# A two-layer decoder trunk: four emission delays, two step spacings of the norms, a shorter weight look-ahead and a fifth lead pair

## The chip, the cores and the metric

The kernel runs on one core of one Trainium2 chip. The metric is the device time of one execution in microseconds: 1768.06 us is the median of three runs before the change (1768.06, 1768.21, 1762.78). Matrix products run on TensorE (PE in the profile, its weight loads PEld), elementwise work on VectorE (DVE), ScalarE (ACT) and GpSimd (POOL); all transfers of weights are queued from SyncE (SP). Each engine works through its own instructions in order.

## The reference, cut to what matters

544 tokens (one prompt of 512 and eight groups of four) pass two layers. Each layer has a token mixer and a SwiGLU feed forward, with a norm ahead of each and behind each, all in float32:

```python
for i in range(DEPTH):                       # DEPTH = 2
    hn = rms_norm(x, mix_pre_norm[i])
    if i % N_MIXERS == 0:
        out, S, cbuf = gdn_mixer(hn, ...)    # gated DeltaNet, layer 0
    else:
        out, hs, cbuf = ssd_mixer(hn, ...)   # Mamba-2, layer 1
    x = x + rms_norm(out, mix_post_norm[i])
    hn = rms_norm(x, ffn_pre_norm[i])
    f = (silu(hn @ ffn_w_gate[i]) * (hn @ ffn_w_up[i])) @ ffn_w_down[i]
    x = x + rms_norm(f, ffn_post_norm[i])
```

D_MODEL is 1024 (8 tiles of 128 features), D_FF 2816 (22 tiles).

## The kernel before

Activations lie with features on the 128 partitions and tokens along the free axis, in two halves of 272 tokens, called hf0 and hf1 here. A float32 operand is split into a high and a low part, and one step of a product over 128 features is three matmuls: high activation by high weight (L238), low activation by high weight (L239), high activation by low weight (L240). Such a step is called a k-step below; the program has 3648 of them.

**Weights** come in pieces of 128x512 (256 KB). `fetch_to` moves a piece in over the SP queue into one of four buffers `wraw`, ACT writes its high part `wh` (L210) and DVE the difference `wl` (L211) into one of five buffer pairs `wspl`. `emit` writes a unit (one output tile of one half): before it writes the product with piece i, it calls `fetch_to(base+i+AHEAD)`, so that pieces up to i+AHEAD-1 have been written into the program by then.

**What sets the order.** The kernel is written out by a planner, `Flow`. It has a virtual time `now`, which each written product moves on, and a list of tasks (Python generators) that run when their due time has come. A task that yields (w, d) is due again d later. The order of writing gives a priority, and a scheduler then places the instructions of each engine; so the numbers in the change are no waits on the chip, they only set the order in which instructions stand on each engine.

**Norms.** Behind the last output tile of a half, `Post.finish` is started. It sums the squares over the features by small matmuls (`ms`, L345), runs a Newton iteration for the inverse root on DVE (L317 to L328, 11 small instructions), spreads the result over partitions (`dg` on DVE L334, `r` on PE L337), and then, for each of 8 tiles: `fw *= r` (DVE L444), `x += fw` (DVE L446, for every third tile POOL), and `pre.square`, which adds the tile's squares for the next norm (ACT, then DVE `acc` L373). Where a feed forward follows, `pre.square` also writes the split of the unnormalized x (`xh` ACT L307, `xl` DVE L308), and the factor r is applied behind the product. `Pre.end` then does sum, Newton and spread for the second norm; where a mixer follows, it writes the normalized tiles `xn` (DVE L409) and their splits `xh`, `xl` (L210, L211). Before hf1's products of the next stage can start, hf1's second norm must have come this far.

**Lead pairs.** A feed forward starts with NL gate and up pairs for hf0 alone, then the same NL pairs for hf1, with their weights fetched and split again; the remaining pairs do both halves with one fetch. While hf0's lead runs, hf1's norms are finished. The gated outputs of the lead lie in the tile `g1`, those of the others in `g2`.

**The DeltaNet mixer** (30 to 440 us) writes its projections for 32 tiles, and per head tasks beside them: `q_task`, `v_task`, `decay`, `scan`, `o_norm`, with start delays in virtual us.

Of the kernel before, what the change touches and what calls it, by code (L numbers as in the profile page):

```python
# [22 lines left out]
NC = SEQ // P  # L23
KFF = 22
NSQ = 5
AHEAD = 5
NL = 4
NZ = 2
ZLAG = 3
SLEAD = 3  # L30
FINE = 12
WIDE = 4
NH0 = 4
PACE = 5.0
LIVE = 3
RAWW = 3 + SEQ + NB * 7
# [48 lines left out]
def _program(nc, tc, io, es):  # L85
# [81 lines left out]
    flow = Flow()  # L167
# [109 lines left out]
    def emit(u, fine=False, wide=False):  # L277
# [7 lines left out]
        for i, s in enumerate(ws):  # L285
            fetch_to(base + i + AHEAD)
            if m < P:
# [92 lines left out]
    class Pre:  # L380
# [16 lines left out]

        def end(self):
            y = rsq(self.ss.sum(), 1e-6)
            yield 0.0, 1.0  # L400
            r = spread(y)
            st.ready[self.hf] = True
            if self.free:
                st.r[self.hf] = sqp.tile([P, H2], F32, tag="sq", name="r", bufs=NSQ)
                S.activation(out=st.r[self.hf], in_=r, func=AF.Copy)
                return
            for k in range(KD):
                t = sqp.tile([P, H2], F32, tag="sq", name="xn", bufs=NSQ)
                V.scalar_tensor_tensor(out=t, in0=self.x[:, k, :], scalar=self.w(k),  # L409
                                       in1=r, op0=ALU.mult, op1=ALU.mult)  # L410
                split(self.xh[:, k, :], self.xl[:, k, :], t)
# [5 lines left out]
    class Post:  # L417
# [17 lines left out]

        def finish(self, hf):
            y = rsq(self.ss[hf].sum(), self.e, None if self.extra is None else self.extra[:, half(hf)])
            yield 0.0, 1.0
            r = spread(y)
            x = st.x[hf]  # L440
            pre = self.pre(hf)
            for k in range(KD):
                f = self.fw(k, hf)
                V.tensor_tensor(out=f, in0=f, in1=r, op=ALU.mult)  # L444
                E = G if k % 3 == 2 else V
                E.tensor_tensor(out=x[:, k, :], in0=x[:, k, :], in1=f, op=ALU.add)  # L446
                pre.square(k)
                yield 0.0, 0.6
            yield from pre.end()

    def ab(tiles, operand, tail):
# [130 lines left out]
    def gdn():  # L582
# [88 lines left out]
        def decay(p):  # L671
            for h in (2 * p, 2 * p + 1):
                d = hd[h]
                gr = t544("gr")
                dma(gr, gd[h].partition_broadcast(P))
                yield 0.0, 1.5
                d.E = tokt("E")
                d.Es = sm.tile([32, 32], F32, tag="Es", name="Es", bufs=6)
                for c in range(NC):
                    V.scalar_tensor_tensor(out=d.E[:, c, :], in0=gr[:, chunk(c)], scalar=Gm[:, c, h:h + 1],  # L680
                                           in1=maskP, op0=ALU.subtract, op1=ALU.min)
                V.scalar_tensor_tensor(out=d.Es, in0=gr[0:32, SEQ:T], scalar=Gm[0:32, 4, h:h + 1], in1=maskS,
                                       op0=ALU.subtract, op1=ALU.min)
                yield 0.0, 1.0
            for d in hd[2 * p:2 * p + 2]:
                S.activation(out=d.E, in_=d.E, func=AF.Exp)
                S.activation(out=d.Es, in_=d.Es, func=AF.Exp)
                d.decay = True
# [190 lines left out]
        def q_after(m, Y):  # L879
            h = m  # L880
            d = hd[h]
            d.q = t544("qT")
            S.activation(out=d.q, in_=Y, func=AF.Silu)
            d.gr = t544("eg")
            dma(d.gr, egd[h].partition_broadcast(P))
            d.el = late.tile([P, 12], F32, tag="el", name="el")
            G.tensor_copy(out=d.el[:, 0:4], in_=d.gr[:, P - 1:SEQ:P])
            G.tensor_copy(out=d.el[:, 4:12], in_=d.gr[:, SEQ + TS - 1:T:TS])
            flow.start(q_task(h), 6.5)

        def q_task(h):
            d = hd[h]
            p, e = divmod(h, 2)
            q, r2 = d.q, pr[p].rk2[:, e, :]
            yield lambda: hasattr(d, "kps")
            qk = dbank("qk")
            for c in range(NC):
                PE.matmul(qk[:, chunk(c)], lhsT=d.k[:, chunk(c)], rhs=q[:, chunk(c)],
                          start=True, stop=True)
            for c in range(NC):  # L900
                V.scalar_tensor_tensor(out=d.E[:, c, :], in0=qk[:, chunk(c)], scalar=r2[:, c:c + 1],
                                       in1=d.E[:, c, :], op0=ALU.mult, op1=ALU.mult)

            sq = t544("qsq")
            S.activation(out=sq, in_=q, func=AF.Square)
            yield 0.9, 0.9
            if e == 0:
                pr[p].qs2 = sm.tile([P, H2], F32, tag="qs2", name="qs2", bufs=3)
            ps = dbank("qss")
            for hf in range(2):  # L910
                r0 = 64 * e + 32 * hf
                PE.matmul(ps[r0:r0 + 32, 0:H2], lhsT=cst[:, C_QQ:C_QQ + 32], rhs=sq[:, half(hf)],
                          start=True, stop=True)
            PE.matmul(ps[0:32, 288:320], lhsT=d.k[:, SEQ:T], rhs=q[:, SEQ:T], start=True, stop=True)
            V.tensor_copy(out=pr[p].qs2[64 * e:64 * e + 64], in_=ps[64 * e:64 * e + 64, 0:H2])
            V.scalar_tensor_tensor(out=d.Es, in0=ps[0:32, 288:320], scalar=r2[0:32, 4:5], in1=d.Es,
                                   op0=ALU.mult, op1=ALU.mult)
            V.tensor_tensor(out=q, in0=q, in1=d.gr, op=ALU.mult)
            yield 0.5, 1.5
            d.qe = True  # L920


        def v_after(m, Y):
            h = m - 16
            v = t544("vT")
            S.activation(out=v, in_=Y, func=AF.Silu)
            flow.start(v_task(h, v), 3.5)

        def v_task(h, v):
            d = hd[h]  # L930
            p, e = divmod(h, 2)
            yield lambda: hasattr(pr[p], "irk")
            irk = pr[p].irk[:, e, :]
            vt = dbank("vtok")
            for c in range(NC):
                PE.transpose(vt[:, chunk(c)], v[:, chunk(c)], ident)
            vs = dbank("vsm")
            PE.transpose(vs[0:32, 0:P], v[:, SEQ:T], ident)
            d.v = tokt("vs")
            V.tensor_tensor(out=d.v, in0=vt.rearrange("p (c k) -> p c k", k=P),  # L940
                            in1=irk[:, 0:NC].unsqueeze(2).to_broadcast([P, NC, P]), op=ALU.mult)
            d.vs = sm.tile([32, P], F32, tag="vs", name="vs", bufs=3)
            V.tensor_scalar(out=d.vs, in0=vs[0:32, 0:P], scalar1=irk[0:32, 4:5], scalar2=None,
                            op0=ALU.mult)
            yield 0.6, 1.2
            yield lambda: hasattr(pr[p], "Dt") and hasattr(d, "qe")
            yield lambda: live[0] < LIVE
            live[0] += 1
            d.o = d.q
            d.left = 2  # L950
            flow.start(scan(h))
            flow.start(sample(h))
# [3 lines left out]
        def ended(h):  # L956
            d = hd[h]
            d.left -= 1
            if d.left == 0:
                live[0] -= 1  # L960
                p = h // 2
                d.ended = True
                if hasattr(hd[h ^ 1], "ended"):
                    flow.start(o_norm(p), 4.0)

        def scan(h):
            d = hd[h]
# [143 lines left out]
        for u in units(start_first(tiles, xop, 1)):  # L1111
            n = names.get(id(u[0]))
            if n is not None and u[1] == 0 and n[0] == "k":
                h = int(n[1])
                if h >= 4:
                    flow.until(lambda: hasattr(hd[h - 4], "ended"))
                if h % 2 == 1 and h < 7:
                    flow.start(decay(h // 2 + 1), 5.0)
            emit(u)
        flow.drain()  # L1120
        conv.close("g")
# [32 lines left out]
    def ffn(layer, last, before, lx, items):  # L1154
        fx = ExitStack()
        ev = pool(f"f{layer}_e", 2, fx, side="right")
        g1 = pool(f"f{layer}_g1", 1, fx, side="right")
        gt = [[[g1.tile([P, NL, H2], F32R, name=f"ga{i}{j}")] for j in range(2)] for i in range(2)]

        def gated(hf, m):  # L1160
            return [(t[0][:, m, :] if m < NL else t[1][:, m - NL, :]) for t in gt[hf]]

# [19 lines left out]
        for m in range(KFF):  # L1182
            tiles += [([io["f_g"][layer, m]], gate_done(m)), ([io["f_u"][layer, m]], up_done(m))]
        for u in units(start_first(tiles, xop, 2 * NL)):
            flow.until(lambda: st.ready[u[1]])
            if u[1] and before is not None:
# [3 lines left out]
                for i in range(2):  # L1190
                    for j in range(2):
                        gt[i][j].append(g2.tile([P, KFF - NL, H2], F32R, name=f"gb{i}{j}"))
                st.updated = False
# [508 lines left out]
```

## Time and profile before

The page of the profile has the busy time of each engine; the trace behind it can be asked for waits and for stretches. The profiled execution is one of its own, with its own time.

| | |
|---|---|
| median of three runs | 1768.06 us |
| the profiled execution | 1778.71 us |
| its span, first to last instruction | 1776.9 us |
| mean granted clock of TensorE | 0.978 |
| DVE / ACT / POOL busy | 1162.0 / 818.0 / 110.2 us |
| weight pieces split, `wl` | 556 |

In rows of a group, "x" is the count, then busy us and the mean ns of one. In a waits row stand the total, the times and the longest. In a windows row each engine has its busy us and, in brackets, its instructions in that stretch; PEclk is the granted clock as a share of full speed. In a timeline row stand the start, the duration, the engine, the line, the instruction, and in square brackets how long the engine was idle before it and what ended that.

### The profile page before, as it was taken

Reading aid. Unit: us, or ns where it says so; the run is one execution under the profiler, and the core shown is the slowest. Engines: PE = TensorE matmul, PEld = TensorE weight load, DVE = VectorE, ACT = ScalarE, POOL = GpSimd, SP = SyncE. Lnnn points to the kernel's source line nnn. Section 1 sums busy time; section 2 is a strip of 40 time slices with the busy share of each in tenths; the row PEclk is TensorE's granted clock in tenths of the full one; section 3 lists DMA queues with packets and bytes.
Section 4 is the critical chain, followed back from the end, with each engine's and each line's share of the span. In section 5 each row is a group of like instructions: output and inputs, shape, how many; then the busy total and the mean of one; then the engine's idle time right before and its main releaser. Section 6 shows DMA issues by size and latency. Waiting matters only on the chain.

```text
span 1776.9 us, 37092 instructions
## 1 busy us (share of the span) xinstructions
PE 1697.0 (96%) x14127; PEld 1612.5 (91%) x14127; DVE 1162.0 (65%) x3069; ACT 818.0 (46%) x1824; POOL 110.2 (6%) x335
## 2 busy tenths in 40 slices
PE   4999999999899999999889999999999999999997
PEld 3888888899799999999777898999998999999996
DVE  6786858455876655324877897978458766665345
ACT  4754654436543333334555555556446433333242
POOL 0112121000000000000001110100001000000000
PEclk8989999999899999999989999999999999999998
DMA  5323323334354432225535544432344544444444
GB/s 141 104 64 100 88 69 96 106 104 145 114 175 145 143 108 90 83 80 143 181 95 150 160 134 137 142 116 74 134 137 137 179 143 141 139 149 131 125 138 130
DMA packets 163124, 220.87 MB, mean 124 GB/s; under 512 B 53185, under 2 KB 66049, under 8 KB 162433
## 3 DMA queue, kind: packets, MB, share of 16 engines
q1 hardware_dynamic: 162944, 218.49, 40.8%
q8 instruction: 111, 1.82, 0.4%
q14 instruction: 69, 0.56, 0.1%
HBM read 197.39 MB, written 21.04 MB: 123 GB/s over the span
## 4 chain that ended last, share of the span: by engine, by line
PE 88%; DVE 6%; ACT 2%; DMA 2%; issue 1%; POOL 0%; SPq 0%; DVEq 0%; ACTq 0%; POOLq 0%
PE mm L238 25%; PE mm L240 25%; PE mm L239 24%; DVE acc L373 1%; PE yd L1495 1%; PE yos L1386 1%; PE yo L1500 1%; PE su L1472 1%; DVE wl L211 1%; PE mm L247 1%; DVE fw L444 1%; PE r L337 1%; PE sc L985 1%; PE ms L345 1%; PE su L573 1%
## 5 line engine op out<-in xcount | busy, mean ns | idle before, releaser
L238 PE MATMUL mm<-xh,wh 128*128 128x272 f32 x2560 | 757.5, 296 | 8.2 <-ACT wh L210 5.1
L240 PE MATMUL mm<-xh,wl 128*128 128x272 f32 x2560 | 752.5, 294 | 2.7 <-DVE wl L211 2.7
L239 PE MATMUL mm<-xl,wh 128*128 128x272 f32 x2560 | 749.8, 293 | 0.0
L211 DVE TENSOR_TENSOR wl<-wr,wh 128x512 fp32r<-128x512 f32 (+1 forms) x556 | 375.8, 679 | 260.0 <-ACT wh L210 247.2
L210 ACT ACTIVATE wh<-wr 128x512 fp32r<-128x512 f32 (+1 forms) x556 | 344.7, 622 | 428.4 <-PE mm L239 377.5
L238 PEld LDWEIGHTS mm<-xh,wh 128*128 128x128 f32 x2560 | 488.8, 191 | 25.9 <-issue 8.0
L240 PEld LDWEIGHTS mm<-xh,wl 128*128 128x128 f32 x2560 | 488.2, 191 | 8.2 <-DVE wl L211 3.8
L239 PEld LDWEIGHTS mm<-xl,wh 128*128 128x128 f32 x2560 | 488.7, 191 | 3.7 <-issue 0.6
L238 PE MATMUL mm<-gb,wh 128*128 128x272 f32 x576 | 166.7, 291 | 0.0
L240 PE MATMUL mm<-gb,wl 128*128 128x272 f32 x576 | 164.9, 289 | 0.4 <-DVE wl L211 0.4
L239 PE MATMUL mm<-gb,wh 128*128 128x272 f32 x576 | 164.3, 288 | 0.0
L544 DVE SCALAR_TENSOR_TENSOR conv<-raw,cw,conv 128x512 f32<-128x512 f32 x144 | 106.8, 742 | 8.7 <-ACT conv L541 8.1
L238 PEld LDWEIGHTS mm<-gb,wh 128*128 128x128 f32 x576 | 108.4, 188 | 1.3 <-ACT wh L210 0.3
L240 PEld LDWEIGHTS mm<-gb,wl 128*128 128x128 f32 x576 | 107.7, 188 | 1.0 <-DVE wl L211 0.6
L239 PEld LDWEIGHTS mm<-gb,wh 128*128 128x128 f32 x576 | 107.8, 188 | 0.4
L1169 ACT ACTIVATE sg<-sg 128x272 f32<-128x272 f32 x88 | 37.7, 431 | 101.2 <-DVE sg L1168 100.6
L446 POOL TENSOR_TENSOR x<-x,fw 128x272 f32<-128x272 f32 x16 | 16.3, 1020 | 1070.4 <-DVE fw L444 561.0
L373 DVE TENSOR_TENSOR acc<-acc,sq 128x272 f32<-128x272 f32 x112 | 50.1, 448 | 45.9 <-ACT sq L366 45.3
L240 PE MATMUL mm<-yh,wl 128*128 128x272 f32 x256 | 73.8, 290 | 2.1 <-DVE wl L211 2.1
L239 PE MATMUL mm<-yl,wh 128*128 128x272 f32 x256 | 74.3, 291 | 1.2 <-DVE yl L308 1.2
L238 PE MATMUL mm<-yh,wh 128*128 128x272 f32 x256 | 73.9, 289 | 0.0
L210 ACT ACTIVATE gb<-sg 128x272 fp32r<-128x272 f32 x72 | 31.1, 432 | 92.8 <-DVE sg L1177 92.8
(399 smaller groups left out, 2428.9 us busy)
## 6 DMA issues: line engine op xcount, KB each, us to landing
wr<-f_d_in SPq DMA_DIRECT2D x110, 256.0 KB
wr<-f_g_in SPq DMA_DIRECT2D x104, 256.0 KB
wr<-f_u_in SPq DMA_DIRECT2D x104, 256.0 KB
wr<-g_w_in SPq DMA_DIRECT2D x64, 256.0 KB
wr<-s_w_in SPq DMA_DIRECT2D x48, 256.0 KB
wr<-s_wo_in SPq DMA_DIRECT2D x44, 256.0 KB
wr<-s_wz_in SPq DMA_DIRECT2D x36, 256.0 KB
ar<-ad SPq DMA_DIRECT2D x32, 272.0 KB
```

Source lines behind the costliest of these rows:

```text
L210: S.activation(out=hi, in_=src, func=AF.Copy)
L211: V.tensor_tensor(out=lo, in0=src, in1=hi.bitcast(F32), op=ALU.subtract)
L238: PE.matmul(ps, lhsT=h[:, k, :], rhs=ah(k0 + k), start=first and k == 0, stop=False)
L239: PE.matmul(ps, lhsT=h[:, k, :], rhs=al(k0 + k), start=False, stop=False)
L240: PE.matmul(ps, lhsT=lo[:, k, :], rhs=ah(k0 + k), start=False, stop=last and k == n - 1)
L247: PE.matmul(ps[0:64], lhsT=w[:, k, :], rhs=a(k), start=j == 0 and k == 0, stop=j == 1 and k == KD - 1)
L337: PE.matmul(r, lhsT=ones[0:TQ, :], rhs=dg.rearrange("p j t -> p (j t)"), start=True, stop=True)
L345: PE.matmul(ps[:, j:j + 1], lhsT=ss[:, q], rhs=sel, start=True, stop=extra is None)
L373: V.tensor_tensor(out=self.acc, in0=self.acc, in1=self.late, op=ALU.add)
L444: V.tensor_tensor(out=f, in0=f, in1=r, op=ALU.mult)
L544: V.scalar_tensor_tensor(out=Y[:, 0:SEQ], in0=R[:, j:j + SEQ], scalar=w[:, j:j + 1], in1=Y[:, 0:SEQ], op0=ALU.mult, op1=ALU.add)
L1169: S.activation(out=t, in_=t, func=AF.Silu)
```

## The change

Six parts, all in what the planner is told:

- AHEAD goes from 5 to 4: a piece is written into the program one piece later.
- NL goes from 4 to 5: each of the two feed forwards fetches and splits one more gate and up pair twice, 4 pieces, 8 in all. The tile `g1` grows by one tile per part and `g2` shrinks by one.
- The yield between the Newton iteration and the spread goes from 1.0 to 3.0 (`NEWTON`) in both norms.
- The yield behind each of the 8 tiles of a norm goes from 0.6 to 1.0 (`TILE`).
- In the DeltaNet mixer the start delays change: `q_task` 6.5 to 9.0, `v_task` 3.5 to 2.5, `o_norm` 4.0 to 3.0, `decay` 5.0 to 3.5.
- No arithmetic changes. The k-steps on PE stay 3648, DVE has 3077 instructions instead of 3069.

```diff
-AHEAD = 5
-NL = 4
+AHEAD = 4
+NL = 5
...
+NEWTON = 3.0
+TILE = 1.0
...
             y = rsq(self.ss.sum(), 1e-6)
-            yield 0.0, 1.0
+            yield 0.0, NEWTON
...
             y = rsq(self.ss[hf].sum(), self.e, None if self.extra is None else self.extra[:, half(hf)])
-            yield 0.0, 1.0
+            yield 0.0, NEWTON
...
                 pre.square(k)
-                yield 0.0, 0.6
+                yield 0.0, TILE
...
-            flow.start(q_task(h), 6.5)
+            flow.start(q_task(h), 9.0)
...
-            flow.start(v_task(h, v), 3.5)
+            flow.start(v_task(h, v), 2.5)
...
-                    flow.start(o_norm(p), 4.0)
+                    flow.start(o_norm(p), 3.0)
...
-                    flow.start(decay(h // 2 + 1), 5.0)
+                    flow.start(decay(h // 2 + 1), 3.5)
```

Two lines are added above line 34, so a line number of the changed kernel is two higher than that of the kernel before (wl is L211 before and L213 after).

**First place: DVE, from the end of the first feed forward into the SSD mixer, before.** `wl` of 128x256 is the last weight piece of the feed forward, `whl` the first piece of the SSD mixer (its narrow dt unit); `xn` and `xl` are hf0's normalized tiles, the 68x4 row is the last instruction of hf0's Newton iteration.

```order
L328 SCALAR_TENSOR_TENSOR ny<-nt,ny 68x4
L334 TENSOR_TENSOR dg<-cst,ny 68x272
L409 SCALAR_TENSOR_TENSOR xn<-x,nrm,r 128x272 x3
L211 TENSOR_TENSOR xl<-xn,xh 128x272
L409 SCALAR_TENSOR_TENSOR xn<-x,nrm,r 128x272 x3
L211 TENSOR_TENSOR xl<-xn,xh 128x272 x5
L409 SCALAR_TENSOR_TENSOR xn<-x,nrm,r 128x272 x2
L211 TENSOR_TENSOR wl<-wr,wh 128x256
L211 TENSOR_TENSOR xl<-xn,xh 128x272 x2
L373 TENSOR_TENSOR acc<-acc,sq 128x272
L211 TENSOR_TENSOR whl<-wr,whl 128x8x32
```

The same place of the changed kernel, from the end of the squares of hf0 on:

```order
L213 TENSOR_TENSOR wl<-wr,wh 128x512
L375 TENSOR_TENSOR acc<-acc,sq 128x272
L213 TENSOR_TENSOR wl<-wr,wh 128x256
L375 TENSOR_TENSOR acc<-acc,sq 128x272
L319 TENSOR_SCALAR nx<-ms 68x4
L213 TENSOR_TENSOR whl<-wr,whl 128x8x32
L320 TENSOR_SCALAR ny<-nx 68x4
L322 TENSOR_SCALAR nh<-nx 68x4
```

The piece of 128x256 and `whl` stood behind fourteen and sixteen of the rows `xn` and `xl`; now both stand ahead of hf0's Newton iteration or within it, and all sixteen `xn` and `xl` come later.

**Second place: DVE in the same stretch, hf1's first norm up to its fifth tile.** The program before:

```order
L211 TENSOR_TENSOR whl<-wr,whl 128x8x32
L334 TENSOR_TENSOR dg<-cst,ny 68x272
L444 TENSOR_TENSOR fw<-fw,r 128x272 x2
L446 TENSOR_TENSOR x<-x,fw 128x272
L211 TENSOR_TENSOR wl<-wr,wh 128x512
L446 TENSOR_TENSOR x<-x,fw 128x272
L211 TENSOR_TENSOR wl<-wr,wh 128x512
L444 TENSOR_TENSOR fw<-fw,r 128x272
L373 TENSOR_TENSOR acc<-acc,sq 128x272
L211 TENSOR_TENSOR wl<-wr,wh 128x512
L444 TENSOR_TENSOR fw<-fw,r 128x272
```

The same of the changed kernel:

```order
L336 TENSOR_TENSOR dg<-cst,ny 68x272
L213 TENSOR_TENSOR wl<-wr,wh 128x512 x2
L446 TENSOR_TENSOR fw<-fw,r 128x272 x2
L448 TENSOR_TENSOR x<-x,fw 128x272 x2
L446 TENSOR_TENSOR fw<-fw,r 128x272 x2
L375 TENSOR_TENSOR acc<-acc,sq 128x272
L448 TENSOR_TENSOR x<-x,fw 128x272
L375 TENSOR_TENSOR acc<-acc,sq 128x272
L446 TENSOR_TENSOR fw<-fw,r 128x272
```

Three weight splits stood among the steps of the norm, and a fourth further down; now two stand ahead of its first step, between `dg` and `fw`, and of the other places only the one further down is kept. From the first `fw` to the last `acc` there are 25 instructions before and 22 now.

**Third place: DVE in the DeltaNet mixer at 106 us, with buffer numbers.** `wl_1511` and `wl_1529` are the two pieces of one projection tile, `conv` the short convolution, `M`, `E`, `kp` steps of the tasks of a head. Before:

```order
L211 TENSOR_TENSOR wl_1511<-wr_1508,wh_1510 128x512
L211 TENSOR_TENSOR wl_1529<-wr_1526,wh_1528 128x512
L544 SCALAR_TENSOR_TENSOR conv_1545<-raw_1544,cw_275,conv_1545 128x512
L730 SCALAR_TENSOR_TENSOR M_1232<-kk_1158,rk2_1081,E_687 128x128 x4
L741 TENSOR_TENSOR kp_1244<-ktok_1153,cf_1242 128x512
```

In the changed kernel the first of the two is `wl_1523` and the second `wl_1703`. The second stands 24 places behind the first, and these rows are the last ahead of it (`vs` is the scaled v of a head, which waits for `vtok` and `vsm` of PE):

```order
L942 TENSOR_TENSOR vs_1497<-vtok_1490,irk_868 128x512
L306 TENSOR_TENSOR kps3_1486<-kps_1484,kps3_1486 32x128
L945 TENSOR_SCALAR vs_1499<-vsm_1495,irk_868 32x128
L323 TENSOR_TENSOR nt_1591<-ny_1590 128x10
L780 TENSOR_TENSOR Us_1042<-Us_1042,cst_80 64x32
L546 SCALAR_TENSOR_TENSOR conv_1539<-raw_1538,cw_275,conv_1539 128x512
L324 TENSOR_TENSOR nt_1591<-nt_1591,nx_1588 128x10
L548 SCALAR_TENSOR_TENSOR conv_1539<-raw_1538,cw_275,conv_1539 128x32
L325 TENSOR_SCALAR nu_1592<-nt_1591 128x10
L213 TENSOR_TENSOR wl_1703<-wr_1700,wh_1702 128x512
```

The second piece of the tile, which stood directly behind the first, now stands behind the convolution and the head's steps, the two waits for PE among them.

## The prediction

> **What bounds the kernel now.** First the page: busy times, and the chain that ended last.
>
> ```profile
> PE 1697.0 (96%) x14127; PEld 1612.5 (91%) x14127; DVE 1162.0 (65%) x3069; ACT 818.0 (46%) x1824; POOL 110.2 (6%) x335
> PE 88%; DVE 6%; ACT 2%; DMA 2%; issue 1%; POOL 0%; SPq 0%; DVEq 0%; ACTq 0%; POOLq 0%
> ```
>
> PE is the bound, and the change gives it the same 3648 k-steps. So only three things can move the time: PE's idle time, the time at a granted clock below full, and what new work adds to either. Next, PE's own waits show who makes it idle.
>
> ```profile
> PE ms L345 <- DVE acc L373: 31.0, 6, 12.0
> PE r L337 <- DVE dg L334: 13.9, 5, 6.4
> PE mm L240 <- DVE wl L211: 5.1, 8, 1.3
> PE mm L238 <- ACT wh L210: 5.1, 5, 2.3
> PE qk L898 <- DVE M L730: 1.1, 1, 1.1
> ```
>
> The sums of the norms (`ms` behind the last `acc`) and their spreads (`r`) take 44.9 us, the weight splits 10.2. The longest `ms` and `r` waits, 12.0 and 6.4, belong to the start of the program, which the change leaves in its order. Then stretches of 25 us, where the loss lies:
>
> ```profile
> core 0: us, PE busy (x) PEld busy (x) DVE busy (x) ACT busy (x) POOL busy (x), PEclk, DMA share, GB/s
> 425.00:450.00 25.00, 20.29 (x161) 19.64 (x160) 21.15 (x56) 17.39 (x41) 1.67 (x2) 0.93 0.32 95
> 450.00:475.00 25.00, 24.14 (x164) 23.47 (x164) 22.21 (x68) 13.80 (x29) 1.81 (x2) 0.86 0.40 127
> 475.00:500.00 25.00, 22.73 (x157) 22.26 (x156) 19.10 (x50) 12.44 (x26) 0.00 (x0) 0.86 0.49 159
> 600.00:625.00 25.00, 25.00 (x198) 24.87 (x197) 15.90 (x38) 8.32 (x16) 0.00 (x0) 1.00 0.44 139
> 850.00:875.00 25.00, 21.55 (x162) 20.49 (x161) 22.48 (x60) 15.55 (x36) 2.86 (x8) 0.96 0.64 195
> 875.00:900.00 25.00, 12.90 (x85) 11.58 (x83) 19.00 (x58) 9.54 (x20) 2.05 (x5) 0.70 0.46 146
> 900.00:925.00 25.00, 23.88 (x169) 22.73 (x168) 19.80 (x54) 16.15 (x31) 0.95 (x4) 0.92 0.26 77
> 1325.00:1350.00 25.00, 22.87 (x179) 22.13 (x178) 22.64 (x63) 14.02 (x31) 2.69 (x2) 1.00 0.44 136
> 1350.00:1375.00 25.00, 23.13 (x181) 22.05 (x180) 21.25 (x60) 15.54 (x33) 2.89 (x2) 1.00 0.43 133
> 1375.00:1400.00 25.00, 22.93 (x174) 21.63 (x173) 23.26 (x61) 15.09 (x30) 0.00 (x0) 1.00 0.56 176
> ```
>
> The row 600:625 is the steady pace: 198 matmuls in 25 us, 0.126 us each, so a k-step of three is 0.38 us. Against it the turn from the DeltaNet mixer to the first feed forward (425 to 500) lacks 112 matmuls, 14 us; the turn into the SSD mixer (850 to 925) lacks 178, 22 us; the turn into the second feed forward (1325 to 1400) lacks 60, 8 us. DVE is busy 19 to 23 of 25 us there against 15.9 in the steady row: in these turns DVE sets PE's pace. The rest is judged turn by turn, and DVE's instructions are priced with these rows:
>
> ```profile
> L211 DVE TENSOR_TENSOR wl<-wr,wh 128x512 fp32r<-128x512 f32 x534 | 366.4, 689 | 204.1 <-ACT wh L210 191.3 <-PE mm L240 1.4 <-PE mm L239 0.8
> L373 DVE TENSOR_TENSOR acc<-acc,sq 128x272 f32<-128x272 f32 x112 | 50.1, 448 | 45.9 <-ACT sq L366 45.3
> ```
>
> So a 272-wide step of a norm costs up to 0.45 us and a weight split up to 0.69.
>
> **Into the SSD mixer: minus 3 us.** The end of hf0's tiles and hf1's norm, on PE and on DVE:
>
> ```profile
> 870.79 0.39 PE L238 MATMUL mm<-xh,wh 128*128 128x272 f32 x1 [1.15 <-ACT wh L210]
> 871.72 0.39 PE L240 MATMUL mm<-gb,wl 128*128 128x272 f32 x1 [0.42 <-DVE wl L211]
> 873.43 0.94 PE L247 MATMUL mm<-xh,whl 128*64 128x272 f32 x3 [0.94 <-DVE whl L211]
> 893.42 1.04 PE L345 MATMUL ms<-cst,acc 128*68 128x1 f32 x8 [9.56 <-DVE acc L373]
> 896.93 0.82 PE L337 MATMUL r<-dg,cst 68*128 68x272 f32 x1 [2.48 <-DVE dg L334]
> ```
>
> ```profile
> 873.29 1.28 DVE L211 TENSOR_TENSOR wl<-wr,wh 128x512 fp32r<-128x512 f32 x2
> 877.12 0.43 DVE L1285 COPY dtT<-mm 64x272 f32<-64x272 f32 x1 [1.41 <-PE mm L247]
> 882.02 0.79 DVE L444 TENSOR_TENSOR fw<-fw,r 128x272 f32<-128x272 f32 x2 [1.26 <-PE r L337]
> ```
>
> The first three PE waits come from the last weight pieces that stand behind the `xn` and `xl` rows (first place of the order). They go. Alone that gains nothing: PE only comes earlier to the gate, hf1's second sum, where it waits 9.56 us. But the late narrow product also holds DVE at `dtT` for 1.41 us, and all of hf1's norm is queued behind it; that wait goes. Then three weight splits leave hf1's norm (second place); back to back two take 1.28 us, so three take 1.9. Two of them now lie in the 1.26 us in which DVE waits for `r` anyway, which they just fill. So the gate comes 1.41 + 1.9 = 3.3 us sooner. What is late next is the tile that POOL adds:
>
> ```profile
> L446 POOL TENSOR_TENSOR x<-x,fw 128x272 f32<-128x272 f32 x16 | 16.3, 1020 | 1070.4 <-DVE fw L444 561.0
> ```
>
> At 1.02 us against 0.45 on DVE it may give back a few tenths; I take 3.0. Ends: 0, if `dtT` waits as long at its new place and POOL's tile or the two splits cover the rest; 6, if the shorter gap also saves part of the stretch of lower clock (875 to 900 had 0.70; a tenth of clock over 25 us is 2.5 us).
>
> **Into the first feed forward: 0.** The wait here, and the two sums on DVE:
>
> ```profile
> 449.10 1.06 PE L345 MATMUL ms<-cst,acc 128*68 128x1 f32 x8 [4.62 <-DVE acc L373]
> 448.61 0.43 DVE L373 TENSOR_TENSOR acc<-acc,sq 128x272 f32<-128x272 f32 x1
> 450.28 0.43 DVE L373 TENSOR_TENSOR acc<-acc,sq 128x272 f32<-128x272 f32 x1
> ```
>
> hf1's first sum, complete at 449.0, has 23 instead of 30 instructions between the first `fw` and its last `acc`, so it is ready some 7 x 0.395 = 2.8 us sooner (two steps in a row took 0.79 above). But hf0's second sum, complete at 450.7, stands one k-step behind it on PE in both programs, and nothing leaves DVE ahead of that one: PE waits there instead. hf1's norm then starts some 3.4 us sooner: the 2.8, and one split of 0.64 fewer between its sum and its first `fw`; its `r` moves along, from k-step 652 to 645. Against that, its second sum stands 20 k-steps earlier on PE (711 to 691), 7.6 us, so it has 4.2 us less cover. In the norm itself stand 9 weight splits instead of 12 and four gate steps fewer, 1.9 + 1.8 = 3.7 us. That leaves 0.5 us of loss, against 2.3 us in which PE waits here for a late weight piece (the longest of the `wh` waits), of which some may go. I take 0, with ends of minus 4.6 (the whole `ms` wait gone) and plus 4.2 (no cover and nothing regained).
>
> **Into the second feed forward: minus 1.** hf1's first sum moves 20 k-steps forward, to directly behind hf0's second (k-step 2617 to 2597), so hf1's norm has 7.6 us more, and the fifth pair lets hf1's lead start 16 k-steps, 6 us, later. The stalls at the start of hf1's lead:
>
> ```profile
> 1374.43 0.39 PE L240 MATMUL mm<-xh,wl 128*128 128x272 f32 x1 [0.64 <-DVE wl L211]
> 1376.74 0.39 PE L240 MATMUL mm<-xh,wl 128*128 128x272 f32 x1 [0.53 <-DVE wl L211]
> 1341.93 0.39 PE L240 MATMUL mm<-yh,wl 128*128 128x272 f32 x1 [1.29 <-DVE wl L211]
> ```
>
> The first two should go, 1.2 us. The third moves: its split now stands ahead of a step that waits for POOL, but DVE's sum of work up to the next weight piece is the same. I take minus 1; ends: minus 7.6, all 60 matmuls that this turn lacks, and plus 4 (hf0's first lead weights stand behind two Newton iterations in place of one, and five or six splits of 0.69 come late).
>
> **The DeltaNet mixer: plus 1.** With AHEAD 4, second pieces of tiles stand behind convolutions and head steps (third place). In the trace:
>
> ```profile
> 106.36 1.27 DVE L211 TENSOR_TENSOR wl<-wr,wh 128x512 fp32r<-128x512 f32 x2
> 121.34 0.69 DVE L940 TENSOR_TENSOR vs<-vtok,irk 128x512 f32<-128x512 f32 x1 [3.45 <-PE vtok L936]
> 114.76 0.39 PE L238 MATMUL mm<-xh,wh 128*128 128x272 f32 x1 [1.44 <-ACT raw L531]
> 118.83 0.43 PE L238 MATMUL mm<-xh,wh 128*128 128x272 f32 x1
> 115.00:130.00 15.00, 15.00 (x248) 12.01 (x249) 8.60 (x30) 4.64 (x10) 2.37 (x9) 0.54 0.28 56
> ```
>
> The pair of splits ends at 107.6, and PE uses the second at 118.8: 11.2 us of slack. Its new place is near 124.5 by the old times, behind `vs` (121.34), the wait for `vsm` and the rows after it: 5.6 us too late. The vtok product and 26 small ones also move ahead of that k-step on PE and take most of this, leaving about 0.6. By the same sums, six other pieces between 72 and 240 us keep 0 to 2 us, one is 1 us late. I take plus 1 for stalls net of the `qk` wait of 1.1 us, which `q_task`'s later start may end. The stretch from 115 to 130, at 0.54 of the clock, loses 15 x 0.46 = 6.9 us. Ends: minus 8, that stretch and the `qk` wait gone; plus 9, one more such stretch and 2 us of stalls.
>
> [...]
>
> **What is added: 0.** Eight pieces, 8 x 0.689 = 5.5 us of DVE, as many splits on ACT, which is busy 12 to 17 of 25 us in these rows, and 2 MB on the SP queue. Per feed forward that is 2.8 us of DVE, beside hf0's and hf1's leads; from 450 to 500 DVE has 50 - 41.3 = 8.7 us free and the transfers moved at most 159 GB/s there against 195 at 850. Without that cover, 5.5. In the steady feed forwards AHEAD 4 costs nothing: DVE has 9 of 25 us free. The queue is passed by nothing but these pieces; POOL keeps its order in the turns.
>
> **Sum.** 1778.71 - 3 + 0 - 1 + 1 + 0 = 1775.7 for the profiled execution. That one stands 10.65 us above the median, so the prediction is 1775.7 - 10.65 = **1765.0**. A measurement here tells about 0.3% (5.3 us) from no change: faster means under 1762.8, slower over 1773.4.
>
> **The rivals.** *Late weights in the mixer (slower).* Place: the seven tight pieces from 72 to 240 us. It decides from the point where the slack goes below zero; price plus 9 in place of plus 1, so 1773, and with a second such stretch 1780. For it: the slack falls from 5 to 14 us to 0 to 2; against: other PE work moves ahead of these pieces too. *Clock stretches go (faster).* If the shorter gaps leave the clock alone in the turns, 425 to 500 regains up to 25 x (0.07 + 0.14 + 0.14) = 8.8 us and 875 to 925 up to 9.5; half of each gives 1756. For it: the third turn has stalls up to 1.29 us and a clock of 1.00; against: the 9.56 us gap shrinks only by a third. *DVE bounds the leads.* Place: both leads, from the point where the 8.7 us free are used up. The 5.5 us of splits are then paid in full: 1770.5. For it: DVE is at 22 to 23 of 25 us in four of the rows; against: the rows right behind them have room. *The change does nothing*: each wait turns into the next one, as at the first sum above, 1768.
>
> **How the numbers follow.** Forecast as summed, 1760 to 1770: 0.38, of it 0.14 faster and 0.24 same. Clock stretches go: 0.26, of it 0.25 faster and 0.01 same. Late weights: 0.24, of it 0.20 slower and 0.04 same. DVE-bound leads or no effect: 0.12, of it 0.07 same and 0.05 slower. Together 0.39 faster, 0.36 same, 0.25 slower. The range 1750 to 1782 takes in the rivals with some 6 us below and 2 above; it leaves out cases in which several ends meet. The forecast's own range is 1760 to 1770.
>
> **What would show it.** In the changed profile: no weight wait at hf0's end into the SSD mixer and PE's waits for hf1's two sums near 9 us in all, with the last one over 3 us sooner after hf0's; a first `ms` wait of about 4 us into the first feed forward, now at hf0's second sum; the second turn's `wl` waits at hf1's lead gone; waits of PE on `wl` between 72 and 240 us of at most 2 us in all. The forecast is wrong if those exceed 3 us, if the granted clock there is below 0.9 in more stretches than before, or if waits on `wl` and `wh` in the leads exceed 10 us in all.

## The result, and the profile after

Eight runs each, in turn on the same chip: 1758.68 us with the change (1753.9 to 1760.84), 1770.07 before (1762.78 to 1778.16). The ratio is 0.9927, 95% interval 0.9903 to 0.9952, so the change takes 0.73% off, some 13 us by the ratio (11.4 by the medians) against the forecast's 3. The profiled execution took 1758.35 us (span 1756.6) against 1778.71; that pair differs by 20.4 us, more than the medians, because the execution profiled before was one of its slowest. Of the runs in the experiments below, two that lay over 1.5% above the fastest run of their kernel (one of the kernel before, one of "AHEAD and q_task") are left out of all means.

The page of the changed kernel, busy times:

```profile
PE 1680.5 (96%) x14127; PEld 1599.9 (91%) x14127; DVE 1165.7 (66%) x3077; ACT 820.1 (47%) x1830; POOL 113.0 (6%) x335
```

and PE's waits after:

```profile
PE ms L347 <- DVE acc L375: 28.2, 6, 11.1
PE r L339 <- DVE dg L336: 13.6, 5, 6.4
PE mm L242 <- DVE wl L213: 9.9, 10, 3.1
```

The count of matmuls is the same, and PE is busy 16.5 us less. Up to 12.7 us of this are clock: span times (1 - granted clock) was 38.9 us in this profile before and is 26.2 after. The waits for sums fall by 2.8 us, and those for `wl` rise from 5.1 to 9.9; the waits for `wh` (5.1) and for `qk` (1.1) are gone from the list. Stretches of 25 us, at the places that answer to those of before (they lie some 20 us earlier from the first turn on):

```profile
core 0: us, PE busy (x) PEld busy (x) DVE busy (x) ACT busy (x) POOL busy (x), PEclk, DMA share, GB/s
75.00:100.00 25.00, 24.51 (x198) 22.49 (x197) 24.84 (x91) 14.52 (x42) 4.32 (x19) 1.00 0.42 108
100.00:125.00 25.00, 24.06 (x450) 21.05 (x449) 21.89 (x81) 16.80 (x42) 8.38 (x23) 1.00 0.40 102
405.00:430.00 25.00, 21.24 (x167) 20.51 (x166) 20.04 (x56) 17.37 (x40) 1.79 (x2) 0.95 0.33 101
430.00:455.00 25.00, 20.56 (x132) 19.18 (x133) 22.97 (x69) 13.38 (x30) 2.85 (x2) 0.84 0.32 101
455.00:480.00 25.00, 24.02 (x191) 23.52 (x190) 20.77 (x52) 14.25 (x29) 0.00 (x0) 1.00 0.64 192
855.00:880.00 25.00, 12.79 (x79) 11.36 (x78) 22.08 (x68) 10.33 (x22) 1.51 (x2) 0.69 0.43 141
1305.00:1330.00 25.00, 22.95 (x173) 22.43 (x173) 20.98 (x59) 14.68 (x33) 2.29 (x2) 0.91 0.37 122
1330.00:1355.00 25.00, 23.87 (x174) 23.05 (x173) 23.51 (x66) 15.05 (x32) 1.75 (x2) 0.96 0.46 137
```

In the mixer, where before had 0.54 of the clock from 115 to 130 us, the clock of this execution is 1.00 throughout; in the gate row (855 to 880) it is as low as before (0.69 against 0.70).

Where the 20 us went, by the timelines: PE comes to the first turn's wait at 425.3 instead of 444.5 us, 19.2 sooner. hf1's second sum, the gate into the SSD mixer, is at 870.8 instead of 893.4, 22.6 sooner. The end is 20.3 us sooner. So nearly all of it lies in the mixer and the stretch ahead of it. Cutting the trace at k-steps (the first one, then 611, 721, 1625, 1745, 2500 and 2690) gives for before and after, with PE idle as the sum of its gaps over 0.15 us:

| | duration before, after | of it PE idle | lost to half clock |
|---|---|---|---|
| up to the first k-step | 37.4, 34.6 | 24.4, 23.3 | 1.9, 0.0 |
| DeltaNet mixer | 394.0, 377.6 | 5.7, 3.5 | 11.7, 0.0 |
| turn into the first feed forward | 61.2, 60.4 | 7.8, 9.0 | 8.5, 5.1 |
| turn into the SSD mixer | 77.5, 75.6 | 15.5, 14.6 | 10.2, 8.5 |
| SSD mixer | 388.1, 390.9 | 7.6, 9.2 | 1.7, 3.4 |
| turn into the second feed forward | 86.7, 84.8 | 5.9, 3.0 | 0.0, 3.4 |

The last column is half the length of the half-clock stretches, an estimate, and a high one: at 78 to 81 us of the kernel before, with PEclk at 0.50, the 128x272 matmuls start 0.226 us apart against 0.126 at full clock, which loses them 0.44 of the time, and where PE also idled less is lost. The stretches of feed forward that are left out take 346.8 and 385.2 us before, 346.3 and 386.5 after. Of the 16.4 us in the mixer 11.7 are half clock by this estimate and 2.2 are waits, and some 2.5 are PE's busy time. One execution says little of the clock: a second profile of the changed kernel has 10.24 us of half clock at the start of the mixer, which then takes 380.7 us.

### The profile page after: what moved, and what is told of

Read it like the earlier page. It is cut to its first block, busy times and chain, and to the rows that moved or that the text cites. A ratio compares the mean times of both kernels' runs of the same rounds, so it can differ in the third digit from the quotient of the medians.

```text
span 1756.6 us, 37084 instructions
## 1 busy us (share of the span) xinstructions
PE 1680.5 (96%) x14127; PEld 1599.9 (91%) x14127; DVE 1165.7 (66%) x3077; ACT 820.1 (47%) x1830; POOL 113.0 (6%) x335
## 5 line engine op out<-in xcount | busy, mean ns | idle before, releaser
L212 ACT ACTIVATE wh<-wr 128x512 fp32r<-128x512 f32 (+1 forms) x564 | 349.3, 622 | 415.5 <-PE mm L241 372.3
L213 DVE TENSOR_TENSOR wl<-wr,wh 128x512 fp32r<-128x512 f32 (+1 forms) x564 | 380.3, 678 | 242.0 <-ACT wh L212 230.1
L240 PE MATMUL mm<-gb,wh 128*128 128x272 f32 x544 | 157.6, 291 | 0.0
L242 PE MATMUL mm<-gb,wl 128*128 128x272 f32 x544 | 155.3, 288 | 0.0
L241 PE MATMUL mm<-gb,wh 128*128 128x272 f32 x544 | 155.0, 288 | 0.0
L240 PEld LDWEIGHTS mm<-gb,wh 128*128 128x128 f32 x544 | 102.2, 188 | 1.3 <-ACT wh L212 0.3
L241 PEld LDWEIGHTS mm<-gb,wh 128*128 128x128 f32 x544 | 102.2, 189 | 0.4
L242 PEld LDWEIGHTS mm<-gb,wl 128*128 128x128 f32 x544 | 101.6, 188 | 0.3
L1179 DVE TENSOR_TENSOR sg<-sg,mm 128x272 f32<-128x272 f32 x88 | 38.4, 436 | 50.6 <-PE mm L242 50.3
```

The costliest lines, as they stand in the source:

```text
L212: S.activation(out=hi, in_=src, func=AF.Copy)
L213: V.tensor_tensor(out=lo, in0=src, in1=hi.bitcast(F32), op=ALU.subtract)
L240: PE.matmul(ps, lhsT=h[:, k, :], rhs=ah(k0 + k), start=first and k == 0, stop=False)
L241: PE.matmul(ps, lhsT=h[:, k, :], rhs=al(k0 + k), start=False, stop=False)
L242: PE.matmul(ps, lhsT=lo[:, k, :], rhs=ah(k0 + k), start=False, stop=last and k == n - 1)
L1179: V.tensor_tensor(out=t, in0=t, in1=ps, op=ALU.mult)
```

## The experiments

Each was run in five rounds beside the kernel before, 12 runs of each kernel (6 of "change again" and of "first turn as before"). Beside the ratio, two numbers of each run are used: **span times mean granted clock**, an estimate of the time that the same run would take at full clock, and **clock loss**, span times (1 - clock). The kernel before has 1737.4, 1737.4 and 1737.7 us for the first in its three sessions (34, 35 and 23 runs), and 30.4, 32.8 and 33.0 for the second; the change has 1731.2 and 24.8. The two are not fully apart: over 231 runs, within one kernel, 1 us more of clock loss goes with 0.2 us less of the first number. Means, with standard errors of 0.4 to 0.8 for the first and 0.5 to 3 for the second:

| kernel | ratio (interval) | span x clock | clock loss |
|---|---|---|---|
| delays alone | 0.9989 (0.9966 to 1.0012) | 1734.2 | 31.9 |
| AHEAD alone | 1.0016 (0.9994 to 1.0038) | 1737.6 | 30.5 |
| spacing alone | 1.0006 (0.9987 to 1.0025) | 1732.8 | 34.9 |
| fifth pair alone | 1.0005 (0.9980 to 1.0029) | 1738.2 | 30.5 |
| delays and AHEAD | 0.9942 (0.9923 to 0.9961) | 1732.3 | 28.0 |
| change, AHEAD 5 | 0.9964 (0.9938 to 0.9989) | 1730.9 | 32.9 |
| change, old delays | 0.9996 (0.9968 to 1.0024) | 1735.5 | 35.1 |
| change, four pairs | 0.9946 (0.9921 to 0.9971) | 1733.3 | 26.9 |
| change again | 0.9926 (0.9897 to 0.9955) | 1731.2 | 26.1 |
| change, first turn as before | 0.9937 (0.9913 to 0.9961) | 1730.1 | 27.8 |
| AHEAD and q_task | 1.0015 (0.9985 to 1.0046) | 1737.5 | 36.2 |
| AHEAD, v_task, o_norm, decay | 0.9953 (0.9936 to 0.9971) | 1732.9 | 28.9 |

**Each part alone.** The four delays:

```diff
-            flow.start(q_task(h), 6.5)
+            flow.start(q_task(h), 9.0)
...
-            flow.start(v_task(h, v), 3.5)
+            flow.start(v_task(h, v), 2.5)
...
-                    flow.start(o_norm(p), 4.0)
+                    flow.start(o_norm(p), 3.0)
...
-                    flow.start(decay(h // 2 + 1), 5.0)
+                    flow.start(decay(h // 2 + 1), 3.5)
```

> Only the four start delays of the DeltaNet mixer change. Theory M (the gain is in the mixer and comes from its delays: the late qk step and the convolution no longer hold PE, so no stretch of half clock follows): 8 to 13 us faster than before, PE idle from 30 to 425 us under 4 us and no half-clock stretch there. Theory A (it comes from the shorter look-ahead): within 2 us of before, the gaps of 1.1, 0.7 and 1.4 us near 74, 76 and 113 us and the half clock behind them stay. Theory T (it comes from the norms' spacing at the turns, as the prediction had it): within 2 us of before.

The look-ahead:

```diff
-AHEAD = 5
+AHEAD = 4
```

> Only AHEAD changes, 5 to 4. Theory A (weight splits stand later, so the mixer's steps pass them): 8 to 13 us faster than before, the mixer without half clock. Theory M: no gain, 0 to 5 us slower, because second pieces come with little slack while the qk wait stays; half-clock stretches in the mixer as before. The recorded prediction: 0 to plus 9, waits on wl between 72 and 240 us.

The spacing:

```diff
-            yield 0.0, 1.0
+            yield 0.0, NEWTON
...
-                yield 0.0, 0.6
+                yield 0.0, TILE
```

> Only the two spacings of the norms change (1.0 to 3.0 behind the Newton iteration, 0.6 to 1.0 behind each tile). Theory T: 3 to 5 us faster than before, with the gate into the SSD mixer 3 us sooner after hf0's tiles. Theories M and A: the mixer is word for word that of before, so at most the 2 to 5 us that the turns gain, and nothing before 425 us.

The fifth pair:

```diff
-NL = 4
+NL = 5
```

> Only NL changes, 4 to 5: a fifth lead pair, 8 more pieces. Recorded prediction: 0, at most 5.5 us slower by the splits. If the fifth pair is what brings the third turn its gain: 1 to 3 us faster, with no wl waits at hf1's lead in the second feed forward. All theories: nothing before 425 us.

None of the four is faster. All three theories of one carrier fall: M, A and T each foretold a gain for one of these. But the two numbers show something else. Delays and spacing each save time at full clock (3.2 and 4.6 us, clear of the errors). The spacing has that eaten by 4.5 us more of clock loss. The delays lose 1.6 us of theirs, within the errors, and the 1.7 us by which their mean time is shorter is not clear of noise either.

AHEAD alone is the harder case. In its profile the mixer's gaps of before have shrunk: the `qk` wait from 1.10 us to 0.27, the one for the raw copy from 1.44 to 0.50.

```profile
73.21 0.57 PE L900 MATMUL qk<-qT,kT 128*128 128x128 f32 x3 [0.27 <-DVE M L732]
110.56 0.39 PE L240 MATMUL mm<-xh,wh 128*128 128x272 f32 x1 [0.50 <-ACT raw L533]
```

PE idles 2.6 us in the mixer instead of 5.7. Yet the mixer less its clock loss takes 382 us in both, and over twelve runs the clock loss is 30.5 us, as in the kernel before. Small gaps alone bring nothing here.

With the delays alone, a wait for ACT's raw copy is longer than before, and half clock follows at once; here PE's row in the timeline of that kernel:

```profile
110.88 0.60 PE L240 MATMUL mm<-xh,wh 128*128 128x272 f32 x1 [2.51 <-ACT raw L533]
```

and its stretches, first the 3.4 us in which most of the wait falls, then the next ten:

```profile
106.84:110.25 3.41, 1.53 (x17) 1.27 (x15) 3.41 (x11) 3.38 (x9) 0.90 (x1) 1.00 0.21 34
110.25:120.49 10.24, 9.61 (x206) 7.66 (x207) 6.44 (x23) 2.82 (x9) 1.01 (x6) 0.50 0.26 50
```

That suggested theory P, tested next: the gain is of two kinds, and the clock's kind goes by PE's idle time within one window of 3.41 us, the step in which the clock records change (the half-clock stretches inside the span of the kernel before last 3.41 to 17.07 us, one to five such steps).

**The parts in pairs, and the change with one part undone.** Delays with AHEAD 4, turns as before:

```diff
-AHEAD = 5
+AHEAD = 4
...
-            flow.start(q_task(h), 6.5)
+            flow.start(q_task(h), 9.0)
...
```

> The four start delays and AHEAD 4 together, without the norms' spacing and without the fifth pair; the mixer's order is that of the change. Theory P (the gain is of two kinds: time at full clock, which adds up over the parts, minus 3.2 by the delays and minus 4.6 by the spacing, and half-clock stretches, which follow where PE's gaps in one 3.4 us window add up to about 1.4 us or more, and which go only if every such gap of the mixer goes): span times clock 1734 to 1735 us, clock loss 25 to 28 us, no mixer gap over 1.3 us, 5 to 8 us faster. Theory S (each part adds its own, delays 0 and AHEAD 0): within 2 us of before.

```diff
-AHEAD = 4
+AHEAD = 5
```

> The change with AHEAD back at 5. Theory P: span times clock as the change's (1730 to 1732 us), but the mixer gap of about 2.5 us at 108 us on ACT's raw copy comes back and a half-clock stretch of about 10 us behind it, clock loss 29 to 32 us: 6 to 8 us faster than before, 4 to 6 slower than the change. Theory A (the look-ahead itself brings the gain): as before, within 2 us. If AHEAD is idle ballast: as the change, 11 to 13 us faster.

```diff
-            flow.start(q_task(h), 9.0)
+            flow.start(q_task(h), 6.5)
...
-            flow.start(v_task(h, v), 2.5)
+            flow.start(v_task(h, v), 3.5)
...
-                    flow.start(o_norm(p), 3.0)
+                    flow.start(o_norm(p), 4.0)
...
-                    flow.start(decay(h // 2 + 1), 3.5)
+                    flow.start(decay(h // 2 + 1), 5.0)
```

> The change with the old start delays of the mixer. Theory P: span times clock 1733 to 1735 us, no mixer gap over 0.6 us (as with AHEAD 4 alone), clock loss 25 to 30 us: 4 to 9 us faster than before. Theory M (the mixer's delays are the gain): within 3 us of before.

```diff
-NL = 5
+NL = 4
```

> The change with four lead pairs. Theory P with the lead alone costing 0.8 us: span times clock 1730 to 1731 us, clock loss 25 us, as the change or 1 us faster. If the fifth pair is needed as cover for hf1's norms once these are spaced wider: 3 us or more slower than the change, with waits on ms or wl at the turns into the feed forwards.

Delays and AHEAD together bring 0.58% where alone they bring 0.11% and nothing: theory S, which adds the single effects, falls. The interaction shows in both numbers, 1732.3 us at full clock against the 1734.2 of the delays alone, and 28.0 us of clock loss against 31.9, each by two to four standard errors. The pair's longest gap in the mixer is 1.23 us, as expected, though in this one execution it fell into a window of small matmuls and 10.24 us of half clock followed. The change with AHEAD 5 hits theory P closely (1730.9 us, the 2.51 us gap at 109 us is back with 10.24 us of half clock behind it, clock loss 32.9 where 29 to 32 was expected). With the old delays theory P misses on all three numbers: the longest gap in the mixer is 1.01 us where none over 0.6 was expected, the time at full clock 1735.5 us, the clock loss 35.1. A stretch of half clock stands there behind a window with no idle time at all, from 170 to 173 us, made mostly of small matmuls; it is the only window of its kind in all the traces. Where the mean loss of 35.1 us falls stays open, and so does a rival: that with the old delays the small products stand in denser bunches, and these cost clock by themselves.

What AHEAD 4 takes out is seen on ACT. In the kernel before, the raw copy that frees the product's buffer stands behind two weight splits (`wh`) and the steps of a head:

```profile
110.47 0.61 ACT L210 ACTIVATE wh<-wr 128x512 fp32r<-128x512 f32 x1
...
111.28 0.61 ACT L210 ACTIVATE wh<-wr 128x512 fp32r<-128x512 f32 x1
...
112.89 0.46 ACT L527 ACTIVATE conv<-mm,cw 128x272 f32<-128x272 f32 x1
...
113.54 0.61 ACT L686 ACTIVATE E<-E 128x512 f32<-128x512 f32 x1
...
114.34 0.37 ACT L531 ACTIVATE raw<-mm 128x272 f32<-128x272 f32 x1
```

With the delays alone, ACT also loads a table in this place, then runs `vT` and a `wh`, and only then comes to the copy:

```profile
107.43 1.28 ACT L928 ACT_TABLE_LOAD   x1
108.72 0.66 ACT L928 ACTIVATE vT<-conv 128x544 f32<-128x544 f32 x1
...
109.57 0.61 ACT L212 ACTIVATE wh<-wr 128x512 fp32r<-128x512 f32 x1
...
110.46 0.37 ACT L533 ACTIVATE raw<-mm 128x272 f32<-128x272 f32 x1
```

With both parts the copies follow their product in one block, with no split between:

```profile
106.49 0.47 ACT L529 ACTIVATE conv<-mm,cw 128x272 f32<-128x272 f32 x1
106.86 0.39 ACT L533 ACTIVATE raw<-mm 128x272 f32<-128x272 f32 x1
107.14 0.37 ACT L537 ACTIVATE raw<-mm 128x240 f32<-128x240 f32 x1
```

The fourteen traces agree on this wait in the DeltaNet mixer: 1.43 to 2.51 us in all five with AHEAD 5; 0.50, 0.50 and 1.02 in the three with AHEAD 4 and the old `v_task`, `o_norm` and `decay`; none over 0.15 in the six with AHEAD 4 and these three tasks sooner.

With four pairs the change is at 0.9946, its interval overlapping that of the change; its time at full clock is 2.1 us longer (errors 0.5 each), where 0 to 1 shorter was expected. Alone the fifth pair brings nothing (0.8 us more at full clock), so what it brings, if anything, needs the other parts.

**Which delays, and can the first turn be had without its cost.** The change was run again, and three variants:

> The change itself once more, beside its variants. Span times clock 1731 us as in its first runs, clock loss 25 us: 10 to 13 us faster than before. If the small clock loss of its first eight runs was luck, it comes out near 30 us and the change is 6 to 8 us faster.

It repeats, 0.9926 with 26.1 us of clock loss.

```diff
-            yield 0.0, NEWTON
+            yield 0.0, 1.0 if (self.kind, self.layer) == (1, 0) else NEWTON
...
-                yield 0.0, TILE
+                yield 0.0, 0.6 if (self.kind, self.layer) == (1, 0) else TILE
...
+        NL = 4 if layer == 0 else 5
```

and the same for the second norm of that turn.

> The change, but at the turn from the DeltaNet mixer into the first feed forward the old spacing (1.0 and 0.6) and four lead pairs; the rest is the change's. If the wider spacing costs 2 to 3 us at that turn (span less half the half-clock time was 52.4 there with the mixer's part alone and 55.2 with the change) and pays only at the turn into the second feed forward: span times clock 1728 to 1729 us, 2 to 3 us faster than the change. If the turns cannot be taken apart: as the change.

The turn itself shortens, from 60.4 and 60.6 us in the change's two profiles to 56.8 here, but the whole is not faster: 0.9937 against 0.9926. At full clock it is 1.1 us shorter, with errors of 0.6 on both, where 2 to 3 was expected. Part went where it was not looked for: the two long feed forward stretches behind the turns take 1 us more each in its profile. No version beats the change clearly.

```diff
-AHEAD = 5
+AHEAD = 4
...
-            flow.start(q_task(h), 6.5)
+            flow.start(q_task(h), 9.0)
```

> AHEAD 4 and only q_task's delay 6.5 to 9.0, turns as before. If the late qk step is what frees PE in the mixer (its wait of 1.1 us and the convolution behind it): most of the pair's gain, 6 to 10 us faster than before. If v_task, o_norm and decay matter: within 3 us of before.

```diff
-AHEAD = 5
+AHEAD = 4
...
-            flow.start(v_task(h, v), 3.5)
+            flow.start(v_task(h, v), 2.5)
...
-                    flow.start(o_norm(p), 4.0)
+                    flow.start(o_norm(p), 3.0)
...
-                    flow.start(decay(h // 2 + 1), 5.0)
+                    flow.start(decay(h // 2 + 1), 3.5)
```

> AHEAD 4 and the other three delays (v_task 2.5, o_norm 3.0, decay 3.5), q_task at 6.5, turns as before. If q_task carries the gain: within 3 us of before, with the qk wait back at 74 us. If the earlier v, o and decay tasks carry it, by spreading the small products over the projections: 6 to 10 us faster, the second half of the mixer (from k-step 300) near 172 us instead of 185.

q_task carries nothing: 1.0015. Its wait for `M` is 0.27 us, but that it is with AHEAD alone too. The three that start sooner carry most of the pair's gain: 0.9953, 1732.9 us at full clock. The mixer from k-step 300 on takes 173.6 us instead of 185.2, and its first part, though it loses 5.1 us to the clock instead of 11.7, takes 210.7 instead of 208.7: small products of the heads have moved forward among the projections. Fewer waits are the smaller part of the 4.5 us at full clock: PE's idle time in the mixer falls by 1.0 us here and 2.2 in the change. The traces show the rest in PE's busy time. The mixer less waits and clock loss takes 372.9 to 374.5 us in the eight traces with the three tasks sooner and 376.3 to 379.6 in the six without, for the same matmuls. Why the same matmuls take less time in this order is not shown.

## Why the prediction was right, and where it was not

The sign and the range of 1750 to 1782 hold. The forecast's own range, 1760 to 1770, was missed by 1.3 us, and that the total came so near is in part luck: the forecast took its 3 us from the turns, while some 10 of the 13 come from the mixer, the term with the wrong sign.

- **The mixer, forecast plus 1.** This step failed. The late second pieces came without harm: PE's one wait for `wl` over 0.15 us before the first turn is this one, where the prediction had 0.6 us for one piece and 1 for another:

```profile
94.22 0.39 PE L242 MATMUL mm<-xh,wl 128*128 128x272 f32 x1 [0.49 <-DVE wl L213]
```

  That is a small miss. The large one is what the step left out. It looked at the new order on DVE and not at ACT, where the shorter look-ahead takes `wh` splits away from ahead of the raw copies, and it had no term for the three tasks that start sooner, which shorten PE's busy time. Delays with AHEAD 4 alone are worth 0.58%, about 10 us of the 13: some 5 each at full clock and of clock loss. The step's lower end, minus 8, did name the half-clock stretch and the `qk` wait that went, but its only reason was `q_task`'s later start, which carried nothing. The rival "late weights" names the right place and is refuted.
- **The clock.** The rival "clock stretches go" looked for them in the turns, where the change's profile still has 10.24 and 17.07 us of half clock. Every kernel with AHEAD 4 and the three sooner tasks has a mean clock loss of 24.8 to 28.9 us, every other one 30.4 to 36.2. The traces place this in the mixer and ahead of it: up to the mixer's end the six traces of the first kind lose 3.7 us on average (0 to 6.8), the eight others 8.7 (0 to 15.4); behind it they lose 24.3 and 22.3. These are single executions. Which gap or product it is that costs the clock in the runs that were not traced stays open, since AHEAD alone has small gaps and the old loss.
- **Into the SSD mixer, forecast minus 3.** Right in mechanism. The last weight pieces no longer stall PE (three waits for `xh` of ACT, 1.31 us in all, stand in the place of their 2.51), and the wait at `dtT` is gone; from the first `fw` to the last `acc` it takes 9.3 us instead of 11.25, 1.95 less, where 1.9 was worked out. The rows after:

```profile
856.07 0.43 DVE L1287 COPY dtT<-mm 64x272 f32<-64x272 f32 x1
861.38 0.77 DVE L446 TENSOR_TENSOR fw<-fw,r 128x272 f32<-128x272 f32 x2
870.24 0.44 DVE L375 TENSOR_TENSOR acc<-acc,sq 128x272 f32<-128x272 f32 x1
870.83 1.04 PE L347 MATMUL ms<-cst,acc 128*68 128x1 f32 x8 [9.67 <-DVE acc L375]
```

  The turn is 1.9 us shorter, not 3. The gate, hf1's second sum, comes 28.0 us behind hf0's second instead of 33.1, so 5 us sooner. But hf0's second sum itself comes 20.2 us behind hf0's first instead of 17.1, which takes 3 us back:

```profile
860.36 0.62 PE L345 MATMUL ms<-cst,acc 128*68 128x1 f32 x8 [0.95 <-DVE acc L373]
842.79 0.62 PE L347 MATMUL ms<-cst,acc 128*68 128x1 f32 x8 [1.18 <-DVE acc L375]
```

  The first row is from before, the second from after. The wider spacing also moves hf0's norm apart, and its second sum stands 8 k-steps (3 us) later on PE, at 1682 instead of 1674; the step did not count that. The piece and the `whl` that moved ahead of hf0's Newton iteration take 0.83 us of DVE, too little for it. PE still waits 9.67 us at the gate, since it also comes there sooner.
- **Into the first feed forward, forecast 0.** Half right. PE waits less for the first sum (2.44 us instead of 4.62), and the wait turns up again right behind it, but not at hf0's second sum: at the first lead weights, which stand behind the norm's steps.

```profile
427.70 1.07 PE L347 MATMUL ms<-cst,acc 128*68 128x1 f32 x8 [2.44 <-DVE acc L375]
431.87 0.60 PE L242 MATMUL mm<-xh,wl 128*128 128x272 f32 x1 [3.11 <-DVE wl L213]
445.71 0.39 PE L242 MATMUL mm<-xh,wl 128*128 128x272 f32 x1 [1.28 <-DVE wl L213]
451.05 0.39 PE L242 MATMUL mm<-xh,wl 128*128 128x272 f32 x1 [0.78 <-DVE wl L213]
```

  The sum of waits is 9.0 us against 7.8. The `wh` wait of 2.27 is gone, the `wl` waits make up for it.
- **Into the second feed forward, forecast minus 1.** Too small at full clock, and the clock took most of it. PE's idle time falls from 5.9 to 3.0 (4.1 in the second profile): the two `wl` waits go (1.17 us), and with them the wait for `r` (1.15) and three weight waits behind (1.54). The third `wl` wait of 1.29 us goes from its place too, but as the step said of DVE's sum of work, it turns up at the next weight piece, where PE waited 0.75 us before:

```profile
1324.69 0.39 PE L242 MATMUL mm<-xh,wl 128*128 128x272 f32 x1 [1.94 <-DVE wl L213]
```

  Less its clock loss the turn is 5 us shorter, 3 of them waits; with it 1.9, since that one gap is followed by 6.8 us of half clock, where before had none. The spacing does this: alone it makes the turn 84.0 us, 82.3 less its clock loss, against 86.7.
- **What is added, forecast 0.** Right: the fifth pair alone is 1.0005.
- **The SSD mixer, no term.** It takes 390.9 us instead of 388.1 (390.2 in the second profile), 1.6 us of it waits and 1.7 half clock. The spacing alone has 390.0.

## What to carry to other kernels

Judge an emission order by time at full clock and by clock loss, each over many runs: delays and spacing alone looked like nothing in the time, though each saved 3 to 5 us at full clock, and the two profiles of the changed kernel differ by a stretch of 10 us at half clock. Shorter gaps of PE did not always shorten the time (with AHEAD alone PE idled 2.6 us in the mixer instead of 5.7, and less its clock loss the mixer took 382 us in both), but where the idle time in one window of 3.41 us came to 1.68 us or more, half clock followed in 70 of 71 cases (the table below). And when weight splits are moved, look at every engine that makes them: here ACT's queue, with a buffer-freeing copy behind the splits, held the mixer's longest gap, 1.44 us.

## What the runs showed of the hardware

Half clock goes with idle time in one window. Over the fourteen traces (before, after and the twelve above) each window of 3.41 us at full clock, from 25 us on, was sorted by PE's idle time in it, and it was counted whether the next window was at half clock:

| PE idle in the window | windows | followed by half clock |
|---|---|---|
| under 0.75 us | 6645 | 1 |
| 0.75 to 1.25 | 123 | 6 |
| 1.25 to 1.68 | 38 | 13 |
| 1.68 and more | 71 | 70 |

In the middle rows idle time alone does not decide. Of the windows with 0.75 to 1.68 us of it, those with fewer than 8 of the large matmuls (128x272) were followed by half clock in 12 of 42 cases, those with 8 to 14 in 7 of 56, those with 15 and more in 0 of 63. The same gap for ACT's raw copy, 1.44 us in the kernel before and 1.43 with the fifth pair alone, lies whole within one window in both. The kernel before, the window with the gap and the stretch behind it:

```profile
112.07:115.48 3.41, 1.97 (x15) 1.56 (x14) 2.62 (x12) 3.39 (x15) 0.57 (x5) 1.00 0.22 34
115.48:129.14 13.66, 13.66 (x225) 11.01 (x226) 8.12 (x27) 3.75 (x7) 1.15 (x4) 0.50 0.30 60
```

and the kernel with the fifth pair alone:

```profile
110.22:113.63 3.41, 1.98 (x16) 1.57 (x14) 2.63 (x13) 3.41 (x15) 0.48 (x5) 1.00 0.22 35
113.63:127.30 13.67, 13.11 (x330) 10.91 (x328) 10.83 (x37) 6.71 (x15) 4.07 (x11) 1.00 0.27 56
```

At 1.97 us busy the next 13.66 us were at half clock, at 1.98 none was, so these two stand at the edge. In the kernel before, the window from 1340.87 us, which holds a gap of 1.29 us and has PE busy for 2.02 us, was followed by full clock too. What ends a stretch is less clear. In the kernel before, a window at half clock with 16 of the large matmuls was followed by full clock (at 78 us), while three with 10, 3 and 4 large ones were followed by half clock again (at 115, 119 and 122 us); but the next, with 7 large and some 120 small ones (at 126 us), was followed by full clock. In each trace all stretches start whole multiples of 3.41 us apart. About half a window of idle time was enough here: 1.68 us or more of the 3.41 was followed by half clock in 70 of 71 cases.
